# Unbroken runs for modulation products and probabilities times V, and six weight tiles

## The chip, the cores and the metric

The kernel runs on one core of a Trainium2 chip. The metric is device time in microseconds (us) of one execution of the whole program. A second way to see the same execution is the trace that the hardware profiler takes: start and duration of every instruction on each engine. PE is the matrix engine (TensorE), PEld its weight loads, DVE the vector engine, ACT the scalar engine, POOL GpSimd, SP the engine whose queue issues nearly all loads from memory.

## The reference, cut to what matters

Two transformer blocks of two layers each work on 256 latent and 256 context tokens of width 1024, all in float32. Every layer has modulation vectors: a condition vector, through a silu, times a wide matrix. Here is the part that the change touches, and where its results go.

```
m_lat = (silu_c @ w_mod[l] + b_mod[l]).reshape(Bsz, N_MOD, 1, D)
m_ctx = (silu_cc @ w_mod[l] + b_mod[l]).reshape(N_MOD, D)
...
h_lat = modulate(rms_norm(x), m_lat[:, 3], m_lat[:, 4])
...
def attend(q, k, v):
    s = jnp.einsum('bqhgd,bkhd->bhgqk', q, k).astype(jnp.float32)
    p = jax.nn.softmax(s, axis=-1).astype(v.dtype)
    return jnp.einsum('bhgqk,bkhd->bqhgd', p, v)
```

`w_mod` has 9216 columns a layer, and the second block has a like matrix of 6144. The mixer of the first layer (`even_mixer`) joins such an attention with a recurrent scan over tokens (RWKV); that of the second layer is windowed attention; those of the second block have differential attention, neighbourhood attention with 64-wide heads, a Fourier mix and gates. Between the mixers stand feed-forward stages, most of the work.

## The kernel before, in words

The program is written as one stream of instructions, with generators woven together by hand (`weave`, `woven`, `chain`, `mixed`), and a scheduler then orders each engine's instructions at compile time from priorities (normally the order of the program), dependencies and the free buffers of each named tile. On the chip each engine follows that fixed order; semaphores hold an instruction until what it reads is there.

**Modulation (`mod_rounds`).** The vectors of 22 of the 30 groups (`ON_PE`) are made on PE in 11 rounds. A round makes four rows of 512 columns, each for two conditions. The stationary operand is a block of 32 columns that holds the condition vectors, the moving operand 512 columns of weights. The four products of one `kc` (one eighth of the contraction) write four blocks of 32 partitions of one PSUM bank (`mod`, one bank): `ps[q:q + 32]` with q = 0, 32, 64, 96. One load brings 512 KB of weights, enough for two of the four. The loads go into tiles of the tag that `k.rtag` names, during the first mixer `rawm`, of which there are four (L685). After eight `kc` ACT copies the bank out (L231), small products turn it (`mod<-arena`) and DVE adds the bias. Each `next` on the generator does one `kc`: two loads and four products. Round 0 is done in two halves at the start of the program, with tiles of its own (`raw0`); the others are side work of the first mixer (`steps_of`), woven between the recurrent scan (`Rwkv`: `keys`, `front`, `inverse`, `mid`, `steps`, `readout`, PSUM tag `rw`), the attention's output projection (`half_out_proj`, tiles `lin<-oa,w`, `lin<-ob,w`) and one another.

**Loads.** `Ker.load` issues on SP's queue. It makes each load wait for a matrix product that lies 72000 columns back in the program (`ahead`); the scheduler makes it wait besides for the tile that it overwrites.

**Probabilities with V (`Pair`).** Attention with 64-wide heads works on two heads at a time. `scores` makes the scores and the softmax, `values` turns the probabilities (`pT`, L585, copied to `PT` by ACT, L586) and multiplies with V. The two heads write partitions 0 to 63 and 64 to 127 of one PSUM tile, first all key blocks of head 0, then all of head 1. There are 8 units in the first mixer and 8 in the third (four with 4 key blocks, four with 2), 8 with 3 key blocks in the second, 4 with 4 in the last. (`Diff`, the 128-wide differential attention, has its own `values` and only shares `pT`.)

A float32 product of the program appears in the trace as two matrix instructions of the same shape, so that one load of modulation weights is four instructions, and one `kc` is eight.

Of the kernel before, what the change touches and what calls it, by code (L numbers as in the profile page):

```python
# [15 lines left out]
P = 128  # L16
KC = 8
# [35 lines left out]
class Ker:  # L53
# [52 lines left out]
    def mm(self, out, l, r, start, stop):  # L106
        i = self.nc.tensor.matmul(out, lhsT=l, rhs=r, start=start, stop=stop)  # L107
        cols = int(np.prod(r.shape[1:])) * (1 if r.dtype == F32R else 4)
        self.work.append(cols + (self.work[-1] if self.work else 0))
        self.at.append(i)  # L110

    def ahead(self, inst):

        if self.work and self.work[-1] > AHEAD:
            self.after(inst, self.at[bisect_left(self.work, self.work[-1] - AHEAD)])
        return inst
# [49 lines left out]

    def load(self, ap, tag=None, bufs=None, after=None):
        t = self.t(ap.shape, *((tag, bufs) if tag else self.rtag))
        i = self.nc.sync.dma_start(out=t, in_=ap)
        self.ahead(i) if after is None else self.after(i, after)  # L170
        return t

# [9 lines left out]
def setup(k):  # L182
    nc = k.nc
    k.vec = k.c([P, NVEC])
    nc.scalar.dma_start(out=k.vec, in_=k.ins["vec"])
    k.lat, k.ctx = Stream(k, 0), Stream(k, 1)
    nc.scalar.dma_start(out=k.lat.X, in_=k.ins["x"])
    cst = k.c([P, 329])
    k.cst = nc.scalar.dma_start(out=cst, in_=k.ins["cst"])
    k.ident, k.bd, k.eye2 = cst[:, 0:128], cst[:, 128:256], cst[:, 256:320]  # L190
    k.sel = cst[:, 320:328]
    k.nzero = cst[:, 328:329]
    k.ones = k.c([P, P])
    nc.vector.memset(k.ones, 1.0)
    k.eps = {}
    for e in (1e-6, 1e-5, 64e-5):
        k.eps[e] = k.c([P, 1])
        nc.vector.memset(k.eps[e], e)
    k.gains = k.c([P, 16])
    for i, n in enumerate(("final_gain", "g_final")):  # L200
        k.ts(k.gains[:, 8 * i:8 * i + 8], k.v(n, 0, 8), -1.0, ALU.mult)
    k.MOD = k.c([P, 30, 8, 2])
    nc.vector.memset(k.MOD[:, 26:30], 0.0)
    k.ready, k.modgen, k.modvec = set(), mod_rounds(k), mod_vectors(k)


def mod_rounds(k):

    nc = k.nc
    cond = k.t([P, 2, 512], "modc", 2)  # L210
    csil = cond[:, 0].rearrange("p (c b w) -> p c b w", c=KC, b=2)
    modb = k.modb = cond[:, 1, 0:480].rearrange("p (g c s) -> p g c s", g=30, c=8)
    nc.scalar.dma_start(out=cond[:, 1, 0:480], in_=k.ins["modb"])
    nc.vector.memset(csil, 0.0)
    cv = k.v("cvec", 0, 32).rearrange("p (b s c) -> p b s c", b=2, s=2)
    for b in range(2):
        k.act(csil[:, :, b, 0:2].rearrange("p c s -> p s c"), cv[:, b], AF.Silu)
    for r, js in [(0, (0, 2)), (0, (1, 3))] + [(r, range(4)) for r in range(1, len(ON_PE))]:
        g, n, step = ON_PE[r], len(js), js[1] - js[0]
        ps = k.p((P, NJ), "mod")  # L220
        for kc in range(KC):
            for a in range(0, n, 2):
                raw = k.load(k.ins["w_modp"][r, kc, :, js[a]:js[a + 1] + 1:step],
                             *(("raw0", 16) if r == 0 else k.rtag))
                for i in range(2):
                    q = 32 * (a + i)
                    k.mm(ps[q:q + 32], csil[:, kc, g // 18], raw[:, i], kc == 0, kc == KC - 1)
            if kc < KC - 1:
                yield
        rows, pr = k.r([P, 512], "s2"), slice(0, 32 * n)  # L230
        nc.scalar.copy(rows[pr], ps[pr])  # L231
        pt = k.p((P, 4, n, 2), "mod")
        for cc in range(4):
            k.mm(pt[:, cc].rearrange("p j s -> p (j s)"), rows[pr, cc * P:(cc + 1) * P], k.sel[pr, 0:2 * n], True, True)
        halves = lambda x: x[:, g:g + 2].rearrange("p v (h c) s -> p c (v h) s", h=2)[:, :, js[0]:js[-1] + 1:step]
        k.add(halves(k.MOD), pt, halves(modb))
        k.ready.update((g + j // 2, j % 2) for j in js)
        yield
# [342 lines left out]
def pT(k, e, nk, PT, qb):  # L581

    pt = k.aux((P, 4, P))
    for kc in range(nk):
        k.nc.tensor.transpose(pt[:, kc], e[:, kc * P:(kc + 1) * P], k.ident)  # L585
    k.nc.scalar.copy(PT[:, :nk, qb * P:(qb + 1) * P], pt[:, :nk])  # L586


class Pair:
# [18 lines left out]

    def values(self):
        k, nk = self.k, len(self.kcs)  # L610
        PTs = []
        for hf in range(2):
            PTs.append(k.t([P, 4, NS], "PT", 3))
            for qb in range(2):
                pT(k, self.e[hf][:, qb], nk, PTs[hf], qb)
            if hf == 0:
                yield
        po = k.aux((P, NS))
        for hf in range(2):
            for i, kc in enumerate(self.kcs):  # L620
                k.mm(po[64 * hf:64 * hf + 64], self.vt(hf, kc), PTs[hf][:, i], i == 0, i == nk - 1)
        k.mark = k.split(po, *self.dst)
        yield

# [33 lines left out]
def weave(main, side, per, rest=True):  # L658

    for _ in woven(main, side, per):  # L660
        pass
    if rest:
        for _ in side:
            pass
# [17 lines left out]
def even_mixer(k, nm, gate, nxt):  # L682
    nc = k.nc
    h, sts = nm.h, nm.sts
    k.wtag, k.rtag = ("w", 5), ("rawm", 4)  # L685
    low = {("gl", s): k.t([P, NS], "low", 1) for s in range(2)}
    for n in ("wl", "al"):
        for s in range(2):
# [76 lines left out]
    pt = k.p((P, 4, P))  # L765
# [38 lines left out]
    def run(main, fill, n=1.0):  # L804
        weave(main, fill, n, False)
# [13 lines left out]
    done = A.readout(ob[1])  # L819
# [464 lines left out]
class Diff:  # L1284
# [23 lines left out]
    def values(self):  # L1308
        k, nk = self.k, len(self.kcs)
        PT = k.t([P, 4, NS], "PT", 3)  # L1310
        for qb in range(2):
            pT(k, self.e[qb], nk, PT, qb)
        yield
        po = k.aux((P, NS))
        for i, kc in enumerate(self.kcs):
            k.mm(po, self.v(kc), PT[:, i], i == 0, i == nk - 1)
        sq = k.r([P, NS], "s1")
        k.act(sq, po, AF.Square)
        p2 = k.aux((P, NS))
        k.mm(p2, k.ones, sq, True, True)  # L1320
        r = k.r([P, NS], "s1")
        neg_rsqrt(k, r, sq, p2, 1.0 / 128.0, 1e-5)
        k.mul(r, r, po)
        hi, lo = self.dst
        k.act(hi, r, AF.Copy, scale=self.sg)
        k.mark = k.stt(lo, r, self.sg, hi, ALU.mult, ALU.subtract)
        yield
# [7 lines left out]
def second_mixer(k, l, nm, outs, gate, nxt):  # L1335
# [69 lines left out]
    q = {i: qk(None, "q2", ocols, 0.125, True, pss[2 * i]) for i in range(2)}  # L1405
    kk = {i: qk(None, "k2", full, 1.0, True, pss[2 * i + 1]) for i in range(2)}
    Vb, vb_steps = values("w_bv_2")
    db = H(k, 4, "br", 8, outs)
    y.extend(k.t([P, ow], "yacc", 4) for _ in range(KC))
# [11 lines left out]
    for _ in range(2):  # L1421
        next(att)
        for _ in range(4):
            next(vb_steps, None)
    Vc, vc_steps = values("w_cv_2")
    weave(att, chain(vb_steps, gates(1, lambda m: y[m]), vc_steps), 0.75 if len(outs) == 2 else 1.6)

# [134 lines left out]
def build(tc, ins, out, dbg=None, stop=None):  # L1562
    with ExitStack() as es:
# [30 lines left out]
        for l in range(2):  # L1594
            outs = [lat] if l else both
            nm = norm_mix(l, odd_first(k, lat, both) if l else even_first(k, both))
            ffn(k, n, ins["ffn_in"][l, 0], ins["ffn_out"][l, 0], Mod(k, 9 * l + 2, mul=0.5), nm,
                modsteps=32)
            dump(f"ffn1_{l}", both)
            n = norm_ffn(l, 1, outs)  # L1600
            (odd_mixer if l else even_mixer)(k, nm, Mod(k, 9 * l + 5), n)
            dump(f"mix_{l}", outs)
            nx = norm_mix2(Between, 0, both) if l else norm_ffn(1, 0, both)
            ffn(k, n, ins["ffn_in"][l, 1], ins["ffn_out"][l, 1], Mod(k, 9 * l + 8, mul=0.5), nx,
                modsteps=0)
            dump(f"ffn2_{l}", outs)
            n = nx
            if stop == f"first{l}":
                return
# [160 lines left out]
```

## Time and profile before

| | us |
|---|---|
| median of 3 runs | 3513.44 (3508.09 to 3514.05) |
| time of the profiled execution | 3510.54 |
| its span, first to last instruction | 3508.8 |
| PE busy | 3386.5 (97% of the span) |
| DVE busy | 2038.4 (58%) |
| ACT busy | 1487.2 (42%) |

The mean granted PE clock was 0.981 of full speed. Busy time says how much of the span an engine worked, not whether something waited for it; a stage in which PE works all the time is limited by PE, one in which it idles by what it waits for. The first mixer's recurrent part lies at about 590 to 1030 us, its attention at 470 to 590, the attention of the other mixers at 1825 to 1895, 2300 to 2450 and 3130 to 3210.

### The profile page before, as it was taken

The page shows a single profiled execution, that of the slowest core. Times are in us where ns is not written, and L with a number is a line of the kernel's source. Part 1 is how long each engine was busy: PE and PEld are TensorE (multiplying, and loading weights), DVE is VectorE, ACT ScalarE, POOL GpSimd, SP SyncE. Part 2 cuts the span into 40 slices and gives each one's busy share as a digit, 9 for nine tenths or more (in the row PEclk, how much of TensorE's full clock was granted, in tenths as well). Part 3 has the DMA queues.
Part 4 walks back from the last instruction along what each step waited for, and adds up shares of the span by engine and source line. Part 5 has one row for each costly group of instructions (what it writes and reads, how often), then busy time and mean ns, then how long its engine had stood idle before and what let it go on. Part 6 is the DMA issues. An engine that isn't in the chain of part 4 may idle for free.

```text
span 3508.8 us, 52267 instructions
## 1 busy us (share of the span) xinstructions
PE 3386.5 (97%) x21258; PEld 2798.9 (80%) x21258; DVE 2038.4 (58%) x3886; ACT 1487.2 (42%) x2611; POOL 6.9 (0%) x20
## 2 busy tenths in 40 slices
PE   8999999879899999999999999999999999999998
PEld 5888866535477888888887998877888888988998
DVE  6753566664763334654377566553466556754776
ACT  4222465543333223422266455653244334554554
POOL 0000000000000000000000000000000000000000
PEclk9999999889999999999999999999999999999999
DMA  7543212457752332453324542222222222334553
GB/s 272 192 145 101 82 55 92 145 182 241 268 179 87 96 96 96 168 192 122 119 68 138 186 148 81 69 82 69 95 97 96 96 96 96 112 109 148 185 185 104
DMA packets 137394, 455.26 MB, mean 130 GB/s; under 512 B 14273, under 2 KB 19905, under 8 KB 136769
## 3 DMA queue, kind: packets, MB, share of 16 engines
q1 hardware_dynamic: 136288, 448.06, 38.0%
q8 instruction: 167, 2.74, 0.3%
q10 hardware_dynamic: 864, 3.85, 0.3%
q14 instruction: 75, 0.61, 0.1%
HBM read 450.81 MB, written 1.05 MB: 129 GB/s over the span
## 4 chain that ended last, share of the span: by engine, by line
PE 90%; DVE 4%; ACT 3%; DMA 2%; issue 1%; SPq 0%; DVEq 0%; ACTq 0%
PE lin L107 72%; PE aux L107 10%; PE rw L107 4%; PE mod L107 3%; PE aux L585 1%; DMA raw<-in_ffn_in 1%; DVE arena L154 1%; DMA raw<-in_w_modp 1%; DVE arena L136 1%; DMA rawm<-in_w_modp 0%; DVE SA L136 0%; ACT arena L157 0%; DVE BL L136 0%; ACT e L157 0%; DVE wf L136 0%
## 5 line engine op out<-in xcount | busy, mean ns | idle before, releaser
L107 PE MATMUL lin<-h,wf 128*128 128x512 f32 (+1 forms) x6240 | 1174.0, 350 | 0.2 <-DVE wf L136 0.2
L107 PEld LDWEIGHTS lin<-h,wf 128*128 128x128 f32 x6240 | 1015.8, 189 | 154.4 <-issue 0.8
L160 ACT CAST wf<-raw 128x1024 fp32r<-128x1024 f32 (+1 forms) x412 | 416.2, 1022 | 698.7 <-PE lin L107 528.6
L107 PE MATMUL lin<-hid,wf 128*128 128x512 f32 (+1 forms) x3456 | 614.6, 339 | 0.0
L107 PEld LDWEIGHTS lin<-hid,wf 128*128 128x128 f32 x3456 | 539.9, 190 | 72.3 <-DVE hid L136 0.6
L136 DVE TENSOR_TENSOR wf<-raw,wf 128x1024 fp32r<-128x1024 f32 (+1 forms) x412 | 489.0, 1189 | 169.3 <-ACT wf L160 157.1
L107 PE MATMUL lin<-h,w 128*128 128x512 f32 (+1 forms) x2328 | 471.2, 358 | 0.0
L107 PEld LDWEIGHTS lin<-h,w 128*128 128x128 f32 x2328 | 382.5, 190 | 69.7 <-issue 10.0
L154 DVE SCALAR_TENSOR_TENSOR arena<-lin,arena 128x256 f32<-128x256 f32 (+2 forms) x339 | 154.1, 481 | 289.3 <-PE lin L107 251.7
L136 DVE TENSOR_TENSOR w<-raw,w 128x1024 fp32r<-128x1024 f32 x160 | 193.8, 1220 | 67.2 <-ACT w L160 66.4
L107 PE MATMUL aux<-h,w 128*128 128x256 f32 x1632 | 215.7, 293 | 17.7 <-ACT h L157 15.3
L107 PEld LDWEIGHTS aux<-h,w 128*128 128x128 f32 x1632 | 208.8, 200 | 27.5 <-ACT h L157 19.6
L136 DVE TENSOR_TENSOR fs<-fs,lin 128x512 f32<-128x512 f32 (+1 forms) x80 | 49.7, 621 | 262.0 <-PE lin L107 262.0
L160 ACT CAST w<-raw 128x1024 fp32r<-128x1024 f32 x160 | 165.2, 1047 | 21.5 <-DMA raw<-in_even_in 5.7
L157 ACT ACTIVATE arena<-arena 128x256 f32<-128x256 f32 (+1 forms) x269 | 102.4, 394 | 119.4 <-DVE arena L154 97.3
L254 DVE CUSTOM_DVE_ANT_0 prod<-rawd,crow,modc 128x1024 f32<-128x1024 f32 x96 | 120.7, 1282 | 54.5 <-DMA rawd<-in_w_modv 53.3
L107 PE MATMUL mod<-rawm,modc 128*32 128x512 f32 x624 | 141.7, 632 | 4.2 <-DMA rawm<-in_w_modp 4.2
L160 ACT CAST hid<-fs 128x512 fp32r<-128x512 f32 (+1 forms) x132 | 72.4, 549 | 128.2 <-DVE fs L136 127.2
L154 DVE SCALAR_TENSOR_TENSOR fs<-lin,arena,fs 128x510 f32<-128x510 f32 (+1 forms) x160 | 98.3, 615 | 47.2 <-ACT fs L157 44.4
L107 PE MATMUL lin<-br,w 128*128 128x512 f32 (+1 forms) x576 | 113.9, 341 | 0.0
L157 ACT ACTIVATE fs<-lin,arena 128x512 f32<-128x512 f32 (+1 forms) x80 | 53.9, 674 | 124.1 <-PE lin L107 124.0
L107 PEld LDWEIGHTS lin<-br,w 128*128 128x128 f32 x576 | 89.6, 189 | 16.2 <-issue 4.7
(252 smaller groups left out, 3292.4 us busy)
## 6 DMA issues: line engine op xcount, KB each, us to landing
raw<-in_ffn_in SPq DMA_DIRECT2D x176, 512.0 KB, 3.9
rawm<-in_w_modp SPq DMA_DIRECT2D x156, 512.0 KB, 5.5
raw<-in_w_up SPq DMA_DIRECT2D x88, 512.0 KB, 3.4
rawd<-in_w_modv SPq DMA_DIRECT2D x64, 512.0 KB, 4.3
raw<-in_ffn_out SPq DMA_DIRECT2D x64, 512.0 KB, 4.5
raw<-in_w_g SPq DMA_DIRECT2D x48, 512.0 KB, 3.4
raw<-in_w_in SPq DMA_DIRECT2D x40, 512.0 KB, 3.4
raw<-in_w_down SPq DMA_DIRECT2D x32, 512.0 KB, 4.3
```

Source lines behind the costliest of these rows:

```text
L107: i = self.nc.tensor.matmul(out, lhsT=l, rhs=r, start=start, stop=stop)
L136: return self.nc.vector.tensor_tensor(out, a, b, op=op)
L154: return self.nc.vector.scalar_tensor_tensor(out, a, s, b, op0=op0, op1=op1)
L157: return self.nc.scalar.activation(out, a, f, **kw)
L160: self.after(self.nc.scalar.copy(hi, src), after)
L254: nc.vector.tensor_tensor_reduce(k.t([P, 1024], "prod", 1), raw, rows[s], 1.0, k.modb[:, g, c, s:s + 1], op0=ALU.mult, op1=ALU.add, accum_ ...
L585: k.nc.tensor.transpose(pt[:, kc], e[:, kc * P:(kc + 1) * P], k.ident)
```

## The change

A helper `run` takes a list of products. It makes the first one wait for everything that it is given (`after`), and gives all others a high priority and an order behind the one before, so that they stand next to each other on PE. Modulation products from round 1 on are collected over two `kc` (eight products, 16 matrix instructions, four loads); in round 0 a run is one load's two products. The products with V of a `Pair` are one run, in the order of key blocks with the two heads taking turns, that waits for all four copies of `PT`. The tiles `rawm` become six.

```diff
+    def run(self, calls, after=()):
+        last = None
+        for c in calls:
+            if last is None:
+                i = self.mm(*c)
+                for a in after:
+                    self.after(i, a)
+            else:
+                with self.tc.high_priority():
+                    i = self.mm(*c)
+                self.tc.add_manual_dep(i.ins, last.ins.name,
+                                       mybir.DependencyInfo(mybir.DependencyClass.NoSync, mybir.DependencyReason.DATA))
+            last = i
...
         ps = k.p((P, NJ), "mod")
+        calls, loads = [], []
         for kc in range(KC):
             for a in range(0, n, 2):
                 raw = k.load(k.ins["w_modp"][r, kc, :, js[a]:js[a + 1] + 1:step],
                              *(("raw0", 16) if r == 0 else k.rtag))
+                loads.append(k.loaded)
                 for i in range(2):
                     q = 32 * (a + i)
-                    k.mm(ps[q:q + 32], csil[:, kc, g // 18], raw[:, i], kc == 0, kc == KC - 1)
+                    calls.append((ps[q:q + 32], csil[:, kc, g // 18], raw[:, i], kc == 0, kc == KC - 1))
+            if r == 0 or kc % 2:
+                k.run(calls, loads)
+                calls, loads = [], []
             if kc < KC - 1:
                 yield
...
-    k.nc.scalar.copy(PT[:, :nk, qb * P:(qb + 1) * P], pt[:, :nk])
+    return k.nc.scalar.copy(PT[:, :nk, qb * P:(qb + 1) * P], pt[:, :nk])
...
-        PTs = []
+        PTs, done = [], []
...
-                pT(k, self.e[hf][:, qb], nk, PTs[hf], qb)
+                done.append(pT(k, self.e[hf][:, qb], nk, PTs[hf], qb))
...
-        for hf in range(2):
-            for i, kc in enumerate(self.kcs):
-                k.mm(po[64 * hf:64 * hf + 64], self.vt(hf, kc), PTs[hf][:, i], i == 0, i == nk - 1)
+        k.run([(po[64 * hf:64 * hf + 64], self.vt(hf, kc), PTs[hf][:, i], i == 0, i == nk - 1)
+               for i, kc in enumerate(self.kcs) for hf in range(2)], done)
...
-    k.wtag, k.rtag = ("w", 5), ("rawm", 4)
+    k.wtag, k.rtag = ("w", 5), ("rawm", 6)
```

## Rows read from the trace of the kernel before

**Rows 1.** The page: engines' busy time (share), then the granted PE clock in 40 slices.
```profile
PE 3386.5 (97%) x21258; PEld 2798.9 (80%) x21258; DVE 2038.4 (58%) x3886; ACT 1487.2 (42%) x2611; POOL 6.9 (0%) x20
...
PEclk9999999889999999999999999999999999999999
```

**Rows 2.** The page: the chain that ended last, share of the span by line.
```profile
PE lin L107 72%; PE aux L107 10%; PE rw L107 4%; PE mod L107 3%; PE aux L585 1%; DMA raw<-in_ffn_in 1%; DVE arena L154 1%; DMA raw<-in_w_modp 1%; DVE arena L136 1%; DMA rawm<-in_w_modp 0%; DVE SA L136 0%; ACT arena L157 0%; DVE BL L136 0%; ACT e L157 0%; DVE wf L136 0%
```

**Rows 3.** Windows: start:end length, busy us of each engine (instructions), PE clock, DMA share, GB/s.
```profile
470.00:590.00 120.00, 119.43 (x610) 90.33 (x609) 77.08 (x188) 69.78 (x154) 0.00 (x0) 1.00 0.18 59
590.00:700.00 110.00, 93.83 (x703) 58.49 (x702) 74.81 (x150) 59.55 (x137) 1.19 (x2) 0.88 0.45 149
700.00:756.00 56.00, 35.46 (x252) 15.02 (x250) 47.89 (x107) 24.54 (x56) 0.00 (x0) 0.83 0.58 193
756.00:900.00 144.00, 141.05 (x1682) 74.59 (x1682) 69.01 (x189) 49.86 (x127) 1.11 (x2) 0.96 0.70 236
900.00:940.00 40.00, 23.86 (x135) 9.19 (x133) 37.87 (x90) 14.87 (x22) 0.00 (x0) 0.81 0.85 329
940.00:1030.00 90.00, 88.31 (x1323) 58.52 (x1324) 47.38 (x152) 29.09 (x63) 0.00 (x0) 0.99 0.52 175
1825.00:1895.00 70.00, 67.66 (x419) 50.49 (x419) 54.91 (x218) 51.11 (x152) 0.00 (x0) 1.00 0.36 121
2300.00:2450.00 150.00, 149.24 (x725) 110.52 (x725) 66.11 (x175) 64.63 (x147) 0.99 (x2) 1.00 0.22 74
3130.00:3210.00 80.00, 78.56 (x501) 64.24 (x501) 38.66 (x93) 37.60 (x74) 0.00 (x0) 1.00 0.40 132
```

**Rows 4.** Groups by form, PE: 590 to 700, 756 to 900, 940 to 1030 (two rows).
```profile
L107 PE MATMUL mod<-rawm,modc 128*32 128x512 f32 x100 | 20.3, 612 | 1.7 <-DMA rawm<-in_w_modp 1.7
...
L107 PE MATMUL mod<-rawm,modc 128*32 128x512 f32 x244 | 64.3, 625 | 0.0
...
L107 PE MATMUL mod<-rawm,modc 128*32 128x512 f32 x108 | 24.2, 605 | 0.0
L107 PE MATMUL mod<-raw,modc 128*32 128x512 f32 x16 | 3.0, 600 | 0.0
```

**Rows 5.** Timeline of PE, 780 to 875: start us, us from first start to last end, instructions.
```profile
780.11 1.05 PE L107 MATMUL mod<-rawm,modc 128*32 128x512 f32 x4
781.09 0.33 PE L107 MATMUL rw<-AL,arena 64*64 64x64 f32 x2
...
854.60 1.06 PE L107 MATMUL mod<-rawm,modc 128*32 128x512 f32 x8
...
870.24 1.92 PE L107 MATMUL mod<-rawm,modc 128*32 128x512 f32 x14
```

**Rows 6.** Waits of SP's queue, 756 to 900: us in total, times, longest.
```profile
SPq L169 <- PE mod L107: 80.4, 34, 6.9
```

**Rows 7.** DMA issues, 756 to 900: count, size, median us from issue to landing.
```profile
rawm<-in_w_modp SPq DMA_DIRECT2D x68, 512.0 KB, 5.4
```

**Rows 8.** Waits of PE, 900 to 940: us in total, times, longest.
```profile
PE mod L107 <- ACT arena L231: 13.9, 1, 13.9
```

**Rows 9.** Windows as in rows 3, but PE's instructions on tile PT alone.
```profile
470.00:590.00 120.00, 18.09 (x96) 1.00 0.18 59
...
1825.00:1895.00 70.00, 22.31 (x93) 1.00 0.36 121
2300.00:2450.00 150.00, 20.23 (x96) 1.00 0.22 74
3130.00:3210.00 80.00, 13.36 (x64) 1.00 0.40 132
```

**Rows 10.** Timeline of PE: products with V of one head (3, 2, 4 key blocks).
```profile
1838.87 1.51 PE L107 MATMUL aux<-PT,VTo 128*64 128x256 f32 x6
...
2405.21 1.08 PE L107 MATMUL aux<-PT,V 128*64 128x256 f32 x4
...
3186.99 1.94 PE L107 MATMUL aux<-PT,V 128*64 128x256 f32 x8
```

More of the change, by code (lines that the diff above doesn't have):

```diff
@@ L110, in mm @@
         self.at.append(i)
+        return i
+    def run(self, calls, after=()):
[11 more added lines that the diff above has]
+            last = i
     def ahead(self, inst):
@@ L168, in load @@
         t = self.t(ap.shape, *((tag, bufs) if tag else self.rtag))
-        i = self.nc.sync.dma_start(out=t, in_=ap)
+        i = self.loaded = self.nc.sync.dma_start(out=t, in_=ap)
         self.ahead(i) if after is None else self.after(i, after)
```

## The prediction

> **What bounds the kernel now.** I read the busy times first: PE works 97% of the span, and its clock stays at the higher of its two levels (2.4 GHz against 1.2) but for slices 8 and 9 [rows 1]. The chain of work that ended last is nearly all PE too, and the two places that this change touches, modulation (`mod`) and the products under `aux`, lie on it [rows 2]. So PE time saved is time saved, wherever PE does not idle already. Where that holds, the view of windows tells, stage by stage [rows 3]. In the attention stages PE is busy 99.5% (470 to 590), 97% (1825 to 1895), 99.5% (2300 to 2450) and 98% (3130 to 3210). In the recurrent part of the first mixer it differs: 756 to 900 and 940 to 1030 are PE's (98%); 590 to 700 is mixed (85%, DVE 68%); 700 to 756 and 900 to 940 are DVE's, the inversion, with PE at 63% and 60% and DVE at 86% and 95%. What PE saves in these last two is worth nothing.
>
> **Modulation, the cost of a run.** The reader should look at how long PE takes for modulation products by the number that stand together [rows 5]. Four instructions, one load, take 1.05 us (the next instruction starts after 0.98). Eight, that is all four blocks of 32 partitions, take 1.06: the other two blocks come free. Fourteen take 1.92, so I price an unbroken run of 16 at 1.92, or 1.85 to the next start (the 0.07 is an overlap with the next). Per load that is 0.46 us in place of 0.98.
>
> From 756 to 900 the products are nearly all in fours: 244 instructions, 61 loads, 64.3 us busy [rows 4]. To the next start that is 61 x 0.98 = 60 us. After the change they are 15.25 runs, 15.25 x 1.85 = 28 us: 32 us less. From 590 to 700 it is 100 instructions, 20.3 us, against 6.25 x 1.92 = 12.0: 8 us less. From 940 to 1030 it is 124 instructions, 27.2 us, against 7.75 x 1.92 = 14.9; less the overlaps of some 20 runs that vanish (1.4) that is 11 us. In the two DVE stages: no gain. Round 0, at the start of the program, keeps runs of one load: no change.
>
> **What the run may cost.** A run stands in PE's fixed order and waits for four loads; everything behind it, the scan's products and with them ACT's and DVE's next work, waits too. What such a wait is like can be seen from 900 to 940: a modulation product whose operand was late held PE for 13.9 us [rows 8]. In 756 to 900 PE waited for no modulation load at all (0.0 in rows 4), so the loads come in time now; but they are tied to PE: SP's queue stood 80.4 us, 34 times, until a modulation product had freed a tile [rows 6], and a load lands 5.4 us after issue [rows 7]. With six tiles and four in a run, two of the next run's loads can be there early and two are issued when a run ends. So runs follow each other at best every 1.85 + 5.4 = 7.3 us. The stage gives each run (144 - 32) / 15.25 = 7.3 us. That is just enough, with nothing to spare. The DMA engines are no nearer limit: 0.70 of 144 us is 101 us of work, a share of 0.84 in 120 us, which is what they show from 900 to 940 (0.85).
>
> The second cost is lost cover. The fours stand between the scan's products now, while ACT and DVE make the operands of the next. With half of that filler gone, PE will wait for them at times. Its upper bound is 32 us of gain (98% busy as now). For the lower I take the nearest stage in which PE does wait: 85% from 590 to 700. PE's remaining 141 - 32 = 109 us at 85% last 128 us, a gain of 16. I take the middle, 24. The clock could fall with the idling: it averages 0.96 at 98% busy and 0.88 at 85% [rows 3]. The Trainium skill has a rule that speaks against the change here ("TensorE: Matmul & The Clock Gate", Why this matters for your kernels): PE that idles between bursts drops to the half clock. Rows 3 agree so far that the stages with an idle PE have the lower mean clock; by the rule the gain of 24 could shrink to the 4 of the first rival, below. By the same shares I take 8 of 11 us from 940 to 1030 and half, 4 of 8, from 590 to 700, where DVE already ends waits. Sum for modulation: 36 us, bounds 16 to 51.
>
> **Products with V.** One head alone writes 64 partitions: 3 key blocks, six instructions, take 1.51 us, 2 take 1.08, 4 take 1.94 [rows 10]. If two heads that take turns run side by side, as the blocks of modulation do [rows 5], a whole unit costs what one head costs now. First mixer: 4 x 1.94 + 4 x 1.08 = 12.1 us against 18.09 [rows 9], 6.0 less. Second: 8 x 1.51 = 12.1 against 22.3 (three of the 96 instructions fall outside that window), 10.2 less. Third: 12.1 against 20.23, 8.1 less. Last: 4 x 1.94 = 7.8 against 13.36, 5.6 less. Together 30 us. The wait for all four copies of `PT` holds head 0 back, but the unit's result waited for head 1 anyway, and three of the four stages have other products to put in front. The second mixer is the doubtful one: 59 us would remain of 70, with 55 of DVE and 51 of ACT [rows 3], 93% for DVE. I take 7 of its 10. Sum 27 us; lower bound 15, if half is lost to waits at the head of a run.
>
> The added tiles, the returned handles and the order within a run cost no instruction. The number of semaphore waits stays: each load and each copy of `PT` was waited for once by its own product and is now waited for once by the head of the run. I set this at nothing.
>
> **Sum.** 36 + 27 = 63 us from 3510.5, the profiled execution's time: 3447.5. The median of the three runs is 2.9 above that execution, which gives 3450.
>
> **Rivals.** *Cover and clock give the modulation gain back.* From 590 to 700 PE waits for DVE and the clock averages 0.88, from 700 to 756 0.83, against 0.96 from 756 to 900 [rows 3]. If 756 to 900 turned into such a stage (85% busy, clock 0.88), its 109 us would last 109 x 0.96 / 0.88 / 0.85 = 140, a gain of 4. With 2 more from 940 to 1030, nothing before, and 20 from the values: 26 us, 3487. For it speaks that mods are 45% of PE's time there; against it, that DVE and ACT are busy only 48% and 35%.
>
> *Heads of runs wait for loads: slower.* Place: the first product of each of 40 runs. Price: a load that lands L us after issue makes a period of 1.85 + L. To lose the 63 us, the 40 runs (ten rounds of four) must each wait 1.6 us on average; to be slower by 0.2%, 1.75 us. If loads come in a burst and queue, an estimate from rows 3 and 7: at the 329 GB/s of 900 to 940 one takes 1.6 us, the third lands after 5.4 + 3.2 = 8.6 us, the period is 10.5, and 756 to 900 takes 160 us, 16 more than now. A wait of 3.2 us in the other 25 runs is 80 us, half of it hidden in DVE's stages. With 27 less from the values that is 3513 + 16 + 40 - 27 = 3542. For it: four loads in one burst queue behind each other. Against: waits for modulation loads are 1.7 us in 590 to 700 and none later [rows 4].
>
> *No effect.* If the order that comes out of the scheduler breaks the runs, or products do not overlap across the sequence, the time stays at 3513. Rows 5 speak against it.
>
> *All of it.* With no wait at all, 51 + 30 = 81 us, and the DVE stages starting earlier: 3430.
>
> **Chances and range.** Forecast (gain 40 to 80) 0.66; cover and clock 0.16; slower 0.09; no effect 0.05; all of it 0.04. Faster by more than 0.2%, about what a measurement of this kernel can tell: 0.86; within 0.2%: 0.05; slower: 0.09. The range goes from 3425 (all of it) to 3497, which takes in most of the first rival (gain 16 and more) and leaves out the slower one, no effect, and the tails.
>
> **What would show it.** Modulation as runs of 16 at 1.9 us in the first mixer, its busy time there about half; units of V at 1.94, 1.51 and 1.08 us with both heads in them, some 30 us less; 756 to 900 shorter by about 24, 700 to 756 and 900 to 940 as long as now. Wrong would show as waits of `mod` for `rawm` loads of 1 us and more at many runs, as PE under 85% after the first inversion, or as a clock under 0.9 there.

## The result, and the profile after

In one comparison on the same chip the changed kernel takes 3465.13 us (median of 4 runs, 3461.58 to 3466.65), the kernel before 3513.18 us (4 runs, 3508.09 to 3514.05): a ratio of 0.9865, 95% interval 0.9848 to 0.9882, 48 us less. The forecast was 63 us less. The profiled execution took 3466.32 us, its span is 3464.2 us.

From the page of the changed kernel, PE's busy time and the granted clock in 40 slices (against [rows 1]):

```profile
PE 3314.8 (96%) x21258; PEld 2779.5 (80%) x21258; DVE 2038.3 (59%) x3886; ACT 1486.6 (43%) x2611; POOL 7.2 (0%) x20
...
PEclk9999999878799999999999999999999999999999
```

PE works 71.7 us less and the span is only 44.6 shorter. The clock is now low in slices 8 to 11, the first mixer.

Windows of the changed kernel over the six stages of the first mixer's recurrent part: up to the first inversion, that inversion, the scan behind it, the second inversion, the scan behind that, the rest up to the feed-forward stage. Columns are length, busy us of PE, PEld, DVE, ACT and POOL (instructions), clock, DMA share, GB/s:

```profile
566.00:696.00 130.00, 108.82 (x852) 69.75 (x850) 84.99 (x179) 76.06 (x176) 1.20 (x2) 0.91 0.41 147
696.00:751.00 55.00, 36.07 (x252) 17.15 (x254) 48.32 (x111) 22.58 (x50) 0.00 (x0) 0.72 0.51 184
751.00:875.00 124.00, 109.48 (x1662) 69.32 (x1659) 69.05 (x188) 49.69 (x127) 1.37 (x2) 0.88 0.73 259
875.00:917.00 42.00, 24.70 (x155) 12.81 (x157) 38.13 (x91) 15.47 (x23) 0.00 (x0) 0.76 0.86 315
917.00:1007.00 90.00, 88.04 (x1339) 66.08 (x1334) 52.22 (x156) 31.61 (x63) 0.00 (x0) 0.87 0.52 177
1007.00:1035.00 28.00, 17.80 (x128) 16.39 (x128) 21.49 (x46) 12.10 (x23) 0.00 (x0) 0.87 0.24 77
```

The same stages of the kernel before, cut near the same instructions (the stages of [rows 3] are rounder):

```profile
572.00:704.00 132.00, 114.74 (x833) 72.48 (x832) 84.85 (x179) 76.47 (x179) 1.19 (x2) 0.90 0.41 135
704.00:756.00 52.00, 32.56 (x220) 14.07 (x220) 47.35 (x107) 20.62 (x44) 0.00 (x0) 0.82 0.55 183
756.00:902.00 146.00, 143.05 (x1696) 75.30 (x1694) 70.49 (x194) 49.86 (x127) 1.11 (x2) 0.96 0.71 239
902.00:940.00 38.00, 21.86 (x119) 8.48 (x117) 36.39 (x86) 14.87 (x22) 0.00 (x0) 0.80 0.84 325
940.00:1028.00 88.00, 86.31 (x1307) 56.52 (x1308) 45.38 (x146) 28.07 (x61) 0.00 (x0) 0.99 0.51 172
1028.00:1063.00 35.00, 25.54 (x197) 24.21 (x197) 28.70 (x57) 16.17 (x28) 0.00 (x0) 0.93 0.34 113
```

Read down: -2, +3, -22, +4, +2, -7, together 491 to 469. The single boundaries are good to a few us only: between the same two products of the scan the first inversion takes 50.1 us in both kernels. In three parts it is safer: 184 to 185 us up to the end of the first inversion, 146 to 124 in the scan behind it, 161 to 160 from there on. Nearly all of the gain in the recurrent part lies in the scan behind the first inversion.

The scan behind the second is no shorter, though modulation takes 10.4 us less of PE there (27.2 to 16.8). Its clock went from 0.99 to 0.87, and products of the next stage moved forward into it. Group `aux<-h,w` of 940 to 1028 before and of 917 to 1007 after:

```profile
L107 PE MATMUL aux<-h,w 128*128 128x256 f32 x3 | 0.9, 343 | 0.0
L107 PE MATMUL aux<-h,w 128*128 128x256 f32 x73 | 11.1, 301 | 0.0
```

The 7 us by which the last stage is shorter are these products.

The recurrent part as a whole, kernel before and changed kernel:

```profile
572.00:1063.00 491.00, 424.05 (x4363) 251.07 (x4363) 313.16 (x765) 206.06 (x458) 2.29 (x4) 0.92 0.56 191
566.00:1035.00 469.00, 384.90 (x4369) 251.50 (x4368) 314.20 (x768) 207.51 (x460) 2.58 (x4) 0.85 0.56 197
```

The group of modulation products, before and after (busy us, mean ns, idle time ahead of them and what ended most of it):

```profile
L107 PE MATMUL mod<-rawm,modc 128*32 128x512 f32 x624 | 141.7, 632 | 4.2 <-DMA rawm<-in_w_modp 4.2
L107 PE MATMUL mod<-rawm,modc 128*32 128x512 f32 x624 | 96.3, 730 | 17.4 <-DMA rawm<-in_w_modp 14.0
```

Four runs in PE's timeline of the changed kernel (start, length; in brackets the idle time ahead; fours before: [rows 5]):

```profile
787.09 3.64 PE L107 MATMUL mod<-rawm,modc 128*32 128x512 f32 x16 [3.14 <-DMA rawm<-in_w_modp]
799.70 3.20 PE L107 MATMUL mod<-rawm,modc 128*32 128x512 f32 x16
807.84 1.92 PE L107 MATMUL mod<-rawm,modc 128*32 128x512 f32 x16
817.43 2.86 PE L107 MATMUL mod<-rawm,modc 128*32 128x512 f32 x16
```

Of the 39 runs 37 are whole, and two came out as 2 and 14 instructions with other products in between. A run takes the forecast 1.92 us at full clock. Of 32 runs that stand alone as sixteen, 14 took longer, 2.3 to 3.64 us: they fell wholly or in part into half-clock time.

PE's busy time on tile `PT` in the four attention stages of the changed kernel (against [rows 9]), and three units in its timeline (against [rows 10]):

```profile
470.00:590.00 120.00, 12.12 (x96) 1.00 0.26 86
1795.00:1865.00 70.00, 12.74 (x96) 0.98 0.36 129
2270.00:2415.00 145.00, 12.13 (x96) 1.00 0.22 78
3090.00:3165.00 75.00, 7.79 (x64) 1.00 0.41 138
```

```profile
476.15 1.95 PE L107 MATMUL aux<-PT,rope 128*64 128x256 f32 x16
491.58 1.08 PE L107 MATMUL aux<-PT,rope 128*64 128x256 f32 x8
...
1799.89 1.52 PE L107 MATMUL aux<-PT,VTo 128*64 128x256 f32 x12 [2.44 <-ACT PT L608]
```

A unit now costs what one head did: 44.8 us in all against 74.0, 29.2 less (forecast 30). The idle 2.44 us ahead of the last one are the wait of a run's head, its first product, for ACT's copy. PE's waits of the changed kernel, whole span (total us, times, longest):

```profile
PE mod L107 <- DMA rawm<-in_w_modp: 14.0, 6, 4.4
...
PE aux L107 <- ACT PT L608: 7.1, 6, 2.4
```

### The profile page after: what moved, and what is told of

The parts are those of the page before. It is cut to its first block, busy times and chain, and to the rows that moved or that the text cites. A ratio compares the mean times of both kernels' runs of the same rounds, so it can differ in the third digit from the quotient of the medians.

```text
span 3464.2 us, 52330 instructions
## 1 busy us (share of the span) xinstructions
PE 3314.8 (96%) x21258; PEld 2779.5 (80%) x21258; DVE 2038.3 (59%) x3886; ACT 1486.6 (43%) x2611; POOL 7.2 (0%) x20
## 4 chain that ended last, share of the span: by engine, by line
PE 69%; DVE 3%; ACT 2%; DMA 1%; issue 0%; DVEq 0%; SPq 0%; ACTq 0%
PE lin L107 59%; PE aux L107 7%; PE rw L107 1%; PE aux L607 1%; PE mod L107 1%; DVE arena L171 1%; DMA raw<-in_ffn_in 1%; DVE arena L153 1%; ACT e L174 0%; ACT arena L174 0%; ACT PT L608 0%; DVE wf L153 0%; DVE inv L153 0%; ACT wf L177 0%; DMA rawo<-in_odd_v 0%
## 5 line engine op out<-in xcount | busy, mean ns | idle before, releaser
L107 PE MATMUL aux<-h,w 128*128 128x256 f32 x1632 | 215.5, 292 | 15.2 <-ACT h L174 14.9
L107 PEld LDWEIGHTS aux<-h,w 128*128 128x128 f32 x1632 | 207.7, 198 | 24.7 <-ACT h L174 19.1
L177 ACT CAST w<-raw 128x1024 fp32r<-128x1024 f32 x160 | 165.3, 1047 | 21.4 <-DMA raw<-in_even_in 6.0
L107 PE MATMUL mod<-rawm,modc 128*32 128x512 f32 x624 | 96.3, 730 | 17.4 <-DMA rawm<-in_w_modp 14.0
```

Source lines behind the costliest of these rows:

```text
L177: self.after(self.nc.scalar.copy(hi, src), after)
```

## The experiments

Medians are set beside 3465 us of the changed kernel; each ratio is to the kernel before, run on the same chip (3510.9 to 3513.2 us). A span is from the profiled execution, and so is "half-clock time", the time within the recurrent part in which the trace grants 0.50, the lower level: 80 us before, 137 after. (The first expectations count it over the whole program: 135 and 186.)

**The two parts by themselves.** `values_only` is the changed kernel without the modulation part and with four tiles:

```diff
-                    calls.append((ps[q:q + 32], csil[:, kc, g // 18], raw[:, i], kc == 0, kc == KC - 1))
-            if r == 0 or kc % 2:
-                k.run(calls, loads)
-                calls, loads = [], []
+                    k.mm(ps[q:q + 32], csil[:, kc, g // 18], raw[:, i], kc == 0, kc == KC - 1)
...
-    k.wtag, k.rtag = ("w", 5), ("rawm", 6)
+    k.wtag, k.rtag = ("w", 5), ("rawm", 4)
```

> Only the products with V are runs; modulation as before, four tiles. If the two halves of the change add up, this is the 22 us that lie between the marks of the changed kernel's attention stages (6 in the first mixer, 5 in the second, 7 in the third, 4 in the last): 3491 us. My prediction's term was 27: 3486. Rival: the heads' waits for the copies of PT eat it in all but the first mixer: 3507.

3492.39 us, ratio 0.9948 (0.9934 to 0.9963): 18.5 us less than before. `mod_only` has the products with V as before:

```diff
-        k.run([(po[64 * hf:64 * hf + 64], self.vt(hf, kc), PTs[hf][:, i], i == 0, i == nk - 1)
-               for i, kc in enumerate(self.kcs) for hf in range(2)], done)
+        for hf in range(2):
+            for i, kc in enumerate(self.kcs):
+                k.mm(po[64 * hf:64 * hf + 64], self.vt(hf, kc), PTs[hf][:, i], i == 0, i == nk - 1)
```

> Only modulation as runs of 16 with six tiles; the products with V as before. If the halves add up: 48 less 22, that is 26 us faster than before, 3487, and as in the changed kernel more time at the half clock than before (186 us against 135). My prediction's term was 36: 3477. Rival: the modulation runs are worth nothing because what PE saves comes back as half clock and waits: 3510.

3485.9 us, 0.9932 (0.9917 to 0.9947): 25.0 us less. The parts come to 43.5 of 48, within the intervals, so no dependence of one on the other can be seen. Forecast were 27 and 36: both terms were too large.

**Loads or length of the run?** `run_per_kc` has runs of eight that wait for two loads; `eight_tiles` has eight weight tiles.

```diff
-            if r == 0 or kc % 2:
-                k.run(calls, loads)
-                calls, loads = [], []
+            k.run(calls, loads)
+            calls, loads = [], []
```

> A run is one eighth of the contraction: eight instructions and two loads, twice as many runs as in the changed kernel. PE's price per load by rows 5 is 0.49 in place of 0.46 us, 4 us more in all. Clock theory (the missing 15 us of modulation's gain went to 50 us more at the half clock, since long stretches of the scan's small products stand between runs): runs come twice as often, the time at the half clock falls below 165 us, and the whole is 3 to 10 us faster than the changed kernel, 3455 to 3462. Load theory (the 15 us went to PE's waits for rawm loads, 14.0 us against 4.2 before): a head waits for two loads, not four; the waits fall below 6 us and the time by as much, with the half clock unchanged at about 186. If neither: 3466 to 3470, the price alone.

3467.46 us, 0.9876 (0.986 to 0.9893), as the changed kernel. Neither theory: PE's waits for loads were 20.0 us against 14.0, half-clock time 148 us against 137. A run of eight in its timeline:

```profile
784.85 1.06 PE L107 MATMUL mod<-rawm,modc 128*32 128x512 f32 x8 [0.16 <-DMA rawm<-in_w_modp]
```

```diff
-    k.wtag, k.rtag = ("w", 5), ("rawm", 6)
+    k.wtag, k.rtag = ("w", 5), ("rawm", 8)
```

> The changed kernel with eight rawm tiles, so that all four loads of the next run have a tile while a run works. Load theory: waits for rawm loads fall from 14.0 to under 5 us and the time by 5 to 9, 3457. Clock theory: the waits may fall, the half clock stays near 186 us and the time within 3 us of 3465.

3474.21 us, 0.9898 (0.9883 to 0.9913), 9 us worse, which neither theory said. PE's waits for loads stayed (13.8 us against 14.0), its idle time in the recurrent part rose from 84 to 91 us, and half-clock time was 145 us. More tiles bring nothing.

**What makes a run cheap?** `unbroken_paired` changes the order inside a run, so that neighbours share a block:

```diff
             if r == 0 or kc % 2:
+                if r:
+                    calls = [calls[j] for j in (0, 1, 4, 5, 2, 3, 6, 7)]
                 k.run(calls, loads)
```

> The changed kernel, with the eight products of a modulation run in another order: blocks 0, 1 of both steps of the contraction, then blocks 2, 3 of both. Runs stay unbroken, wait for the same four loads and stand at the same places, but only two of the four blocks of 32 partitions stand side by side at a time. Theory one: the saving is that of the four blocks standing side by side. Then a run takes 2.9 to 3.8 us in place of 1.92, and the time is 20 to 35 us above the changed kernel: 3485 to 3500; half-clock time in the first mixer falls from 137 towards 100 us as PE's work grows. Theory two: unbroken sequences save by themselves, whatever the order of blocks: a run takes 1.9 to 2.1 us, the time stays within 5 us of 3465.

3470.03 us (3463.52 to 3474.29), 0.9874 (0.9859 to 0.9888): the second theory. A run in its timeline:

```profile
823.73 1.94 PE L107 MATMUL mod<-rawm,modc 128*32 128x512 f32 x16
```

The four blocks overlap although two products each for blocks 0 and 1 stand ahead of those for blocks 2 and 3. My reason for the price ("all four blocks side by side") was too narrow. `no_forcing` collects and waits, but leaves the rest to the scheduler:

```diff
-                with self.tc.high_priority():
-                    i = self.mm(*c)
-                self.tc.add_manual_dep(i.ins, last.ins.name,
-                                       mybir.DependencyInfo(mybir.DependencyClass.NoSync, mybir.DependencyReason.DATA))
+                i = self.mm(*c)
```

> The changed kernel without what holds a run together: products are collected as before and the first waits for everything, but the others get no high priority and no order behind the one before; the scheduler places them as it likes. Theory one: collecting alone is enough, since products that become ready together come out next to each other: runs of 16 as now, time within 5 us of 3465. Theory two: the forced order is what does it: other work is put between the products, the groups fall apart to fours and eights at 1.05 us, modulation's gain of about 21 us is lost and part of that of the values: 3480 to 3500.

3474.76 us (3473.8 to 3485.42), 0.9888 (0.9871 to 0.9904), between the theories: 29 runs stand alone as sixteen (32 in the changed kernel), a few break, and some 10 us are lost. Collecting does most of it.

**The tiles alone.**

```diff
-    k.wtag, k.rtag = ("w", 5), ("rawm", 4)
+    k.wtag, k.rtag = ("w", 5), ("rawm", 6)
```

> The kernel before with six weight tiles in place of four and nothing else. Theory one: loads did not limit the kernel before (PE waited 1.7 us for them from 590 to 700 us and none after), so nothing changes: within 5 us of 3513. Theory two: earlier loads let the modulation products move forward and the stages of the inversion, in which PE idles, take more of them: 5 to 15 us faster, and then part of the change's gain is that of the tiles.

This is the only edit to the kernel before. 3507.55 us, 0.9986 (0.9977 to 0.9996): 5 us less, between the theories and under the 0.2% bound. The first inversion took more of the modulation work: 98 of its instructions for 78 between the same two products of the scan. Runs of sixteen with four tiles were not tried, so how much of `mod_only`'s 25 us belongs to the tiles stays open.

The clock in this run bears on what follows. Its recurrent part:

```profile
573.00:1065.00 492.00, 424.69 (x4371) 253.88 (x4369) 313.76 (x766) 206.85 (x461) 2.48 (x4) 0.89 0.55 188
```

Beside the kernel before, the length, PE's busy time and its idle time (67 us) are the same, and no product became cheaper; yet half-clock time is 106 us for 80. So the rise to 137 in the changed kernel need not come from shorter modulation alone, and here 25 us more at the half clock made the part no longer.

**Does more PE work hold the clock?** `filler` puts zeros into the modulation bank, `filler_spread` into a spare bank between the scan's products:

```diff
+    zeros = k.c([P, 32])
+    nc.vector.memset(zeros, 0.0)
...
             if r == 0 or kc % 2:
                 k.run(calls, loads)
                 calls, loads = [], []
+            elif kc:
+                k.run([(ps[32 * q:32 * q + 32], zeros, k.vec[:, 0:512], False, False) for q in range(4)])
```

> The changed kernel with extra products: at every even step of the contraction of each round from round 1 on, except the first, four more products (a stationary block of zeros, the constant vectors as moving operand, no load and no wait) go to the four blocks of the modulation bank. They add only zeros, so the result is that of the changed kernel; the extra work is about 30 groups of eight matrix instructions, 0.93 us to the next start at full clock, 28 us of PE time inside the first mixer. Theory one, the clock: modulation's 68 us less of PE work were given back in part because PE ran 137 us of the first mixer at half clock in place of 80; if thinner PE work is what lets the clock fall, thicker work holds it up: half-clock time in the mixer under 100 us, and the whole costs much less than 28 us, at most 10 (3465 to 3475). Theory two, the waits: PE idles because operands of the scan come late, the clock does not follow this work: half-clock time stays at 130 to 145 us, and the part of the 28 us that falls where PE sets the time, some 20 us, is paid in full: 3483 to 3495.

3489.75 us (3486.95 to 3491.57), 0.9931 (0.9916 to 0.9946): the second theory. Half-clock time stays at 130 us, and 25 us of the 28 are paid. The trace shows why this says less than I meant: 20 of the 30 extra groups stand right behind a run, which makes the run longer and the stretch between runs no fuller. Hence the other place, in `mm` during the scan:

```diff
+        if self.scan is not None and 16 <= cols // 4 <= 128:
+            self.scan += 1
+            if self.scan % 36 == 0:
+                n, self.scan = self.scan, None
+                pf, last = self.aux(), i
+                for q in (0, 32):
+                    j = self.mm(pf[q:q + 32], self.zeros, self.vec[:, 0:512], True, True)
...
+                    last = j
+                self.scan = n
```

> The changed kernel with 49 extra groups of four matrix instructions in the first mixer, each put right behind every 36th small product of the scan: zeros times the constant vectors, into two blocks of a spare bank that nothing reads, so the result stays. That is 49 x 0.98 = 48 us of PE work, about the 52 us that modulation gave up, spread between the small products as the fours of the kernel before were; the earlier filler stood mostly right behind the runs of 16. Theory one: what kept the clock up was PE work spread through the scan: half-clock time in the mixer falls from 137 to under 105 us, PE's idle time from 84 to under 70, and the whole costs under 25 us (below 3490). Theory two: the clock does not follow extra work wherever it stands: half-clock time stays over 120 us and the work is paid at the rate of the first filler (25 us for 28), some 42 us: 3500 to 3515.

3501.78 us (8 runs, 3494.05 to 3505.41), 0.997 (0.9959 to 0.998): 37 of 48 us paid, half-clock time 113 us, idle time 81 us. Neither theory's numbers. By stage it is clearer; windows of `filler_spread`, the scan behind the first inversion, the second inversion, the scan behind it:

```profile
762.00:908.00 146.00, 129.94 (x1784) 74.72 (x1780) 75.15 (x209) 50.40 (x128) 1.11 (x2) 0.94 0.73 248
908.00:947.00 39.00, 26.06 (x116) 11.74 (x114) 31.74 (x71) 15.56 (x23) 0.00 (x0) 0.68 0.80 300
947.00:1039.00 92.00, 91.47 (x1377) 57.84 (x1375) 48.18 (x149) 28.52 (x60) 0.00 (x0) 1.00 0.49 171
```

In the two scans the clock is back at 0.94 and 1.00 (0.88 and 0.87 in the changed kernel, 0.96 and 0.99 before); in the inversion it is not. Only the first scan can be put down to the filler: in the other versions with runs, without such spread products, its clock was 0.83 to 0.91. The scan behind the second inversion has 0.82 to 1.00 among them. `eight_tiles` and `unbroken_paired`, which have no filler:

```profile
933.00:1013.00 80.00, 77.37 (x1335) 60.23 (x1331) 47.35 (x146) 29.34 (x60) 0.00 (x0) 1.00 0.58 198
926.00:1010.00 84.00, 80.85 (x1312) 61.10 (x1305) 52.88 (x156) 32.64 (x64) 0.00 (x0) 0.96 0.56 190
```

`unbroken_paired` has as many modulation and projection products in this scan as the changed kernel, which took 90 us for it at 0.87. So part of what the changed kernel lost there is the clock of its profiled execution, and the filler shows nothing about it. As a repair the filler fails in any case: it cost 37 us.

**Half of the loads.**

```diff
-        calls, loads = [], []
+        calls, loads, raws = [], [], {}
...
-                raw = k.load(k.ins["w_modp"][r, kc, :, js[a]:js[a + 1] + 1:step],
-                             *(("raw0", 16) if r == 0 else k.rtag))
-                loads.append(k.loaded)
+                if r == 0 or kc % 2 == 0:
+                    raw = k.load(k.ins["w_modp"][r, kc, :, js[a]:js[a + 1] + 1:step],
+                                 *(("raw0", 16) if r == 0 else k.rtag))
+                    loads.append(k.loaded)
+                    raws[a] = raw
+                raw = raws[a]
```

> The changed kernel with half of the modulation weights left out: from round 1 on the products of an odd step of the contraction use the tiles of the even step before, so a run waits for two loads, not four, and 20 MB less are moved. The vectors that come out are wrong; the work of PE, ACT and DVE is the same. Theory one: late loads at the heads of runs cost part of modulation's missing 12 us: PE's waits for these loads fall from 17 us to under 3 and the time by 5 to 12 us (3453 to 3460). Theory two: they cost nothing that another wait does not take over: waits for loads go, the time stays within 4 us of 3465.

3449.81 us (3444.99 to 3466.37), 0.9842 (0.9815 to 0.9869): the median is 15 us lower, more than the first theory's 5 to 12; the interval still overlaps that of the changed kernel. (The loads left out are 40 MB, not 20: 80 loads of 512 KB.) Windows of the two inversions and of the last scan:

```profile
693.00:746.00 53.00, 38.48 (x318) 19.69 (x318) 46.77 (x110) 21.46 (x46) 0.00 (x0) 0.81 0.38 123
...
867.00:914.00 47.00, 31.25 (x206) 18.16 (x207) 44.06 (x106) 18.66 (x28) 0.00 (x0) 0.85 0.28 90
914.00:985.00 71.00, 66.67 (x1214) 53.22 (x1213) 44.60 (x145) 26.24 (x55) 0.00 (x0) 0.88 0.39 128
```

The reader should see where the gain sits: the inversions take more of PE's work (38.5 and 31.3 us for 36.1 and 24.7), and the last scan, relieved of it, lasts 71 us in place of 90. About half of that relief is modulation (14.9 to 5.8 us), the other half output projection (`lin<-ob,w`, 14.2 to 4.7 us) that now stands in the second inversion. PE's waits for the loads shrank only from 14.0 to 7.9 us. Modulation in the first inversion, changed kernel and `half_loads`:

```profile
L107 PE MATMUL mod<-rawm,modc 128*32 128x512 f32 x96 | 17.9, 884 | 8.7 <-DMA rawm<-in_w_modp 8.7
L107 PE MATMUL mod<-rawm,modc 128*32 128x512 f32 x160 | 20.3, 648 | 3.9 <-DMA rawm<-in_w_modp 2.8 <-DVE arena L153 1.1
```

So the loads keep modulation out of this inversion, four runs of it. What it is about them is not shown. In the changed kernel the DMA engines are busy only 0.51 of its 55 us (0.86 in the second inversion, where `half_loads` adds a single run), and SP's queue stands most of it until a modulation product frees a tile:

```profile
SPq L186 <- PE mod L107: 37.9, 8, 11.4
```

Half the loads also make six tiles reach twice as far, and the scheduler's order changes with them.

**Forcing more into the inversions.**

```diff
-    run(woven(A.inverse(), side, 1), chain(mixed(out_a, 99), mod), 3)
-    run(woven(A.mid(), side, 2), chain(mixed(out_a, 99), mod), 1.5)
-    run(woven(A.steps(), side, 1), mod, 3)
+    run(woven(A.inverse(), side, 1), chain(mixed(out_a, 99), mod), 5)
+    run(woven(A.mid(), side, 2), chain(mixed(out_a, 99), mod), 1)
+    run(woven(A.steps(), side, 1), mod, 1.5)
...
-    run(woven(B.inverse(), side, 0.7), mod, 1)
+    run(woven(B.inverse(), side, 0.7), mod, 2)
```

> The changed kernel with side work shifted into the two inversions, in which DVE sets the time and PE idles: 5 steps of modulation for 3 during the first inversion, 1 for 1.5 and 1.5 for 3 in the two stages behind it, 2 for 1 during the second. Theory one: idle PE time there takes two to four more runs of 16, the PE-bound stages lose them: 4 to 8 us faster (3457 to 3461). Theory two: loads limit what these stages can take (0.85 of the DMA engines' time is used from 900 to 940 in the kernel before), the runs wait, and the time stays or rises by up to 5 us.

3490.17 us (3476.26 to 3493.63), 0.9934 (0.9911 to 0.9957): 25 us worse than the changed kernel, beyond even the second theory. Its group of modulation products:

```profile
L107 PE MATMUL mod<-rawm,modc 128*32 128x512 f32 x640 | 103.3, 754 | 31.2 <-DMA rawm<-in_w_modp 27.8 <-issue 3.2
```

PE now idles 31.2 us ahead of these products, 27.8 of it for loads, and what stands behind them in PE's order waits with them; half-clock time is 167 us. But the inversions did not get more modulation. Its groups in the first and in the second:

```profile
L107 PE MATMUL mod<-rawm,modc 128*32 128x512 f32 x84 | 15.9, 890 | 9.2 <-DMA rawm<-in_w_modp 9.2
L107 PE MATMUL mod<-rawm,modc 128*32 128x512 f32 x80 | 12.3, 755 | 8.8 <-DMA rawm<-in_w_modp 8.8
```

That is 84 and 80 instructions for 96 and 80 in the changed kernel. So the run shows what late loads at the heads cost, and leaves open whether the inversions could take more of full loads.

**The wait for the copies.** `values_lagged` issues a unit's run one unit later (`pipe`, with `values` cut in two):

```diff
...
         yield from u.scores()
+        if held is not None:
+            yield from held[0].product(*held[1])
+            held = None
         if prev is not None:
-            yield from prev.values()
+            held = yield from turned(prev)
         prev = u
-    yield from prev.values()
+    if held is not None:
+        yield from held[0].product(*held[1])
+    held = yield from turned(prev)
+    if held is not None:
+        yield from prev.product(*held[1])
```

> The changed kernel, in which the run of products with V of a pair of heads is issued one unit later, behind the scores of the unit after next; transposes and copies stay where they are. The run then finds its four copies done long ago. Theory one: the heads of these runs wait for ACT's copies (7 us in the second mixer), which is what the products with V miss of their 27 us: the waits go and the time falls by 4 to 8 us (3457 to 3461). Theory two: the wait only moves, to the transposes or to what reads the result: within 3 us of 3465.

3452.06 us (3445.32 to 3456.0), 0.9831 (0.9816 to 0.9846): 13 us less than the changed kernel, the first theory and more, and the fastest version here that computes everything. In the profiles 7.6 us of it lie in the three later mixers; the recurrent part of the first, which holds hardly any of these products, is 6 us shorter too, and no run says why. PE's wait for the copies in the second mixer (1795 to 1870 us) is down from 6.8 us to 0.8:

```profile
PE aux L107 <- ACT PT L608: 0.8, 1, 0.8
```

## Why the prediction was right, and where its sizes were off

**Prices of runs: right.** 1.92 us for sixteen modulation instructions, 1.95, 1.52 and 1.08 us for units of V, 29.2 us less on `PT`.

**Modulation: 36 us forecast, 25.0 measured alone, 22 in the profile.** The mechanism was right; the mis-sized terms are "4 of 8" from 590 to 700 and "8 of 11" from 940 to 1030. From 756 to 900 the forecast of 24 came true (22). Up to the end of the first inversion nothing was gained (184 to 185 us): cheaper modulation was brought forward there, 224 instructions for 188, and took 38.5 us for 39.4. From the second inversion on 161 us became 160: modulation took 13.6 us less of PE there, but all other products, as many as before, took 10.4 more, while half-clock time rose from 22 to 52 us and PE's idle time by 2. The prediction let the clock fall only in a rival; its own sum had no term for it in these stages.

The same as one sum over the recurrent part: 39 runs at 1.92 us would be 74.9 us busy, 66.8 less than before. They were 96.3, so 21.4 were not saved; PE's other instructions took 6.2 more (modulation fell by 45.4, all of PE by 39.2); PE's idle time rose by 17.2 (66.95 to 84.1). 66.8 - 21.4 - 6.2 - 17.2 = 22.

**The rival "cover and clock": its mechanism is there, at part of its price.** It said PE 85% busy and the clock at 0.88 behind the first inversion; it is 88% and 0.88, and a clock under 0.9 there I had named as a sign of a wrong forecast. Yet the stage lost 22 us, not 4. The step of the rival that fails is the factor 0.96 / 0.88 on all of PE's work: the products other than modulation took 76.1 us there, 77.7 before. The slower clock shows in modulation alone, 33.4 us for 14 runs that would be 26.9 at 1.92. The rule of the Trainium skill ("TensorE: Matmul & The Clock Gate", Why this matters for your kernels), that PE idling between bursts falls to half clock, agrees with the trace in direction: idle time up by 17 us, mean clock of these stages from 0.92 to 0.85. It is not the whole: in `six_tiles_only` the half-clock time rose by 25 us with the idle time unchanged. How the 11 us of shortfall divide between clock and waits stays open.

**The rival "heads of runs wait for loads": not as a burst, and far smaller.** PE's waits for these loads rose from 4.2 to 14.0 us, far from the 63 that would have cancelled the gain. (Of the 4.2 us, 2.5 lie from 700 to 756, a stage that rows 4 leave out; "none later" overlooked them.) More tiles did not help. The loads do keep modulation out of the first inversion (`half_loads`); "in the two DVE stages: no gain" held for these loads and not in itself.

**Products with V: 27 us forecast, 18.5 measured alone.** The first mixer gave the 6 us forecast (from the first product of its units to the last: 110.1 to 104.2 us). Between the starts of the feed-forward stages the second mixer gave 4.1 us for 7 (485.3 to 481.2), the third 6.7 for 8.1, the last 4.2 for 5.6. The mis-sized term is "7 of its 10" for the second mixer: of the 7.1 us that PE waits for copies of `PT` in the changed kernel, 6.8 lie there (2.3 before), so the stage had too little to put in front. In the third and the last PE hardly waits for the copies; why each falls 1.4 us short is not shown. With the run one unit later (`values_lagged`) the same three stages give 7.6, 9.4 and 5.6.

**No cost of waits and tiles:** six tiles alone are worth some 5 us (1 to 8 by the interval), a gain that the sum did not have.

## What to carry to other kernels

Products on separate column blocks overlap when they stand in one sequence, so collect them; then move the sequence to where its operands are long done, since a wait at its head holds the whole engine. When filler work gets cheaper, price what it covered: here PE's idle time rose by 17 us and its mean clock fell from 0.92 to 0.85. Do not take a lower clock as a loss in proportion, though: ask which products got longer. In a stage in which PE idles, find what keeps work out of it (here the loads of modulation), and look in the trace whether a reordering has put more there.

## What the runs showed of the hardware that I had not expected

The clock can stay low while PE is full. Windows of the changed kernel, the end of the second inversion and the stretch behind it:

```profile
911.50:918.40 6.90, 4.65 (x131) 3.00 (x132) 6.73 (x10) 5.79 (x8) 0.00 (x0) 0.99 0.23 81
918.40:942.30 23.90, 23.26 (x285) 15.38 (x277) 4.64 (x15) 7.96 (x17) 0.00 (x0) 0.50 0.26 93
```

PE was 97% busy for 23.9 us at a clock of 0.50; 233 of its 285 instructions were the scan's small products, the others 32 of modulation and 20 of the output projection. And two products each for blocks 0 and 1 of PSUM partitions do not hold up those for blocks 2 and 3 behind them: the paired order takes 1.94 us for sixteen instructions, against 1.92 in turns. When all eight instructions of one head stood ahead of the eight of the other, as in the first unit of the kernel before, the unit took longer than the 1.95 us in turns:

```profile
477.22 2.92 PE L107 MATMUL aux<-PT,rope 128*64 128x256 f32 x16 [0.29 <-ACT PT L586]
```
